# Values, indexer keys and head weights in one step of 336 columns, and wider indexer visits, in a two-layer streaming encoder

## Chip, cores and metric

The kernel runs on one core of one Trainium2 chip. The metric is the device time of one execution in microseconds (us), of which three runs were taken. The engines are named as in the profile: PE is TensorE, PEld its weight loads, DVE is VectorE, ACT is ScalarE, SP issues the loads and stores.

## What is computed

The program is one inference step of an encoder with two layers, for 256 tokens of a prompt and 8 x 16 sample tokens that share the weights (384 tokens). Cut to what matters here:

```python
for i in range(2):                                  # layers
    z  = rmsnorm(x, norm_mix) @ w_in                # one input projection, 2048 -> all groups
    q, k, v, qi, ki, wi, gates, glu, pool = split(z)
    ki = rope(ki)                                   # indexer key: 64 columns, one per token
    qi = rope(qi)                                   # indexer queries: 16 heads of 64
    logits = einsum('qhd,sd->qhs', qi, ki) / 8
    score  = einsum('qhs,qh->qs', relu(logits), wi) / 4     # wi: 16 head weights per token
    idx = top_k(where(visible, score, -inf), topk)  # chunks of 64 tokens are causal
    o_att = attention(q, k[idx], v[idx]) * silu(g_att)
    x += concat(o_att, conv(glu), pool(pool)) @ w_out
    x += sigmoid(rmsnorm(x, norm_ple) @ w_ple_gate) * (p[i] @ w_ple_proj)
y = rmsnorm(x)                                      # k, v, ki of each layer are outputs too
```

## The kernel before, in words

**Weights in pieces.** All weights pass once through the chip, in a list of pieces of 128 partitions x 1024 columns that the loop `w_dma` sends over SP's queue. `w_split` turns each piece into two: ScalarE copies it into `whi` (line 114, fp32r, the rounded part) and VectorE subtracts that from it into `wlo` (line 115). Activations are held in the same two parts, so every product takes three matmuls, lines 238, 239 and 240 in `mm3`. `w_ahead` keeps some pieces split and loaded ahead of the one in use.

**Main steps.** `ORDER` lists the steps of a layer. Each entry is an `mstep`: 48 matmuls into one bank with the tag "mm", weights stationary, the 384 tokens (320 for the indexer queries "qi") as the moving columns, over 2 pieces. The result is read by the evacuation in `pending` after the first half of the following step. The first entry, `t0`, holds the 64 columns of ki and the 16 of wi, padded to 128; `ev_t0` (line 384) scales, rotates and stores them with the columns on the partitions. The values are another kind of step, `v_step` (line 840): here the activations are stationary and 256 columns of `w_in` move, so the result has tokens on the partitions; it takes 144 matmuls over 4 pieces and three "mm" banks (lines 851 to 853).

**What runs between.** After every half step, `pump` lets each track go on to its next `yield`. `att_gen` (line 621) is the attention: it turns wi to tokens on the partitions (two transposes and two matmuls with a constant `em` that is loaded in each layer), then takes the indexer scores in visits. In the first prompt tile (64 queries whose scores count, 128 keys) a visit is one pair of heads, in the second tile (128 queries, 256 keys) too, both on line 651; for the sample it is one of the eight requests (line 691). Each matmul has 64 rows of the array, the two heads of a pair in its two row halves, and each writes a bank of its own with the tag "sd". ScalarE takes the relu, VectorE multiplies by the head weight and adds (line 660). `conv_gen` (its taps on VectorE, line 483) is another track. Of the eight accumulation banks four carry "mm" and four "sd".

**The start.** Ahead of layer 0, `ple_proj` projects the embeddings: 4 pieces, 96 matmuls of 384 columns into "sd" banks (their inputs are `phi` and `plo`), copied out by VectorE and ScalarE in turn (line 303 is ScalarE's). The squares for the norm (`square_gen`, line 199) write buffers that held `phi` and `plo`. `stats` (line 152) adds up the squares with three small matmuls (line 156) and spreads the result with transposes (line 170); it is called on after the first two steps of `ORDER`.

**Who sets the order.** The program's order is not the order on the engines: the framework schedules each engine's list ahead of time, with a simulated timeline and the banks and buffers as limits. TensorE's list then runs strictly in that order.

## Time and profile before

| | |
|---|---|
| median of three runs (lowest to highest) | 1517.2 us (1515.77 to 1517.27) |
| the profiled execution | 1517.27 us, its span 1515.4 us |
| TensorE matmuls | busy 1493.7 us, 99% of the span, 8839 instructions |
| VectorE | busy 1000.8 us, 66% |
| ScalarE | busy 667.1 us, 44% |
| loads and stores | 216.10 MB, mean 143 GB/s |

The busy time of an engine is the time in which at least one of its instructions ran. In the rows of the timeline a matmul's duration is longer than the distance to the next one, since two overlap; the distance between starts is what a matmul costs. The chain is followed back from the last instruction to what released it, or to the instruction before it on its engine. The share of a line in the chain tells where the time lies, and the list of waits tells for what an engine stood still.

### The profile page before, as it was taken

How to read it: one execution, taken by the hardware profiler on the slowest of the kernel's cores; microseconds unless marked ns; L12 is line 12 of the kernel's file. 1: busy time of each engine (PE TensorE's matmuls, PEld its weight loads, DVE VectorE, ACT ScalarE, POOL GpSimd, SP SyncE). 2: the span in 40 equal slices, each digit the busy share in tenths (PEclk: the TensorE clock that was granted, in tenths of full speed). 3: DMA queues.
4: the chain of work that ended last, by engine and by line, in shares of the span. 5: the costliest groups of instructions: out<-in, count | busy, mean ns of one | idle time of the engine just before them, and what ended most of it. 6: DMA issues, size and time to landing. Idle time of an engine off the chain costs nothing.

```text
span 1515.4 us, 22769 instructions
## 1 busy us (share of the span) xinstructions
PE 1493.7 (99%) x8839; PEld 1449.6 (96%) x8839; DVE 1000.8 (66%) x1775; ACT 667.1 (44%) x1163; POOL 3.6 (0%) x36
## 2 busy tenths in 40 slices
PE   8999999999999999999999999999999999999995
PEld 8999999999999999999999999999999999999995
DVE  7887979767466444466678797978655654445554
ACT  7653333347543333444445334344554343345441
POOL 0000000000000000000000000000000000000000
PEclk9999999999999999999999999999999999999997
DMA  9654443433446444455454444443344644444432
GB/s 339 207 154 132 149 130 113 137 110 98 135 150 205 126 126 128 132 181 175 152 172 153 134 144 129 127 138 112 98 119 131 201 137 131 128 125 125 126 111 84
DMA packets 84684, 216.10 MB, mean 143 GB/s; under 512 B 11232, under 2 KB 40800, under 8 KB 84576
## 3 DMA queue, kind: packets, MB, share of 16 engines
q1 hardware_dynamic: 84576, 214.65, 45.8%
q8 instruction: 69, 1.13, 0.3%
q14 instruction: 39, 0.32, 0.1%
HBM read 200.70 MB, written 13.91 MB: 142 GB/s over the span
## 4 chain that ended last, share of the span: by engine, by line
PE 98%; DVE 1%; ACT 1%; DMA 0%; SPq 0%; issue 0%; DVEq 0%
PE mm L238 29%; PE mm L240 29%; PE mm L239 29%; PE sd L651 1%; PE sd L238 1%; PE sd L240 1%; PE sd L239 1%; PE mm L851 1%; PE mm L852 1%; PE mm L853 1%; PE sd L715 1%; PE sd L742 1%; PE sd L691 1%; DVE xr L998 0%; DMA wraw<-in_wpp_dram 0%; PE sd L779 0%
## 5 line engine op out<-in xcount | busy, mean ns | idle before, releaser
L114 ACT ACTIVATE whi<-wraw 128x1024 fp32r<-128x1024 f32 (+1 forms) x341 | 357.7, 1050 | 631.6 <-PE mm L239 469.7
L115 DVE TENSOR_TENSOR wlo<-wraw,whi 128x1024 fp32r<-128x1024 f32 (+1 forms) x341 | 412.9, 1211 | 229.6 <-ACT whi L114 227.6
L238 PE MATMUL mm<-xh,whi 128*128 128x384 f32 (+1 forms) x752 | 252.5, 336 | 0.5 <-ACT whi L114 0.5
L238 PE MATMUL mm<-nh,whi 128*128 128x384 f32 (+1 forms) x752 | 252.4, 336 | 0.0
L240 PE MATMUL mm<-nh,wlo 128*128 128x384 f32 (+1 forms) x752 | 250.5, 333 | 0.0
L240 PE MATMUL mm<-xh,wlo 128*128 128x384 f32 (+1 forms) x752 | 250.5, 333 | 0.0
L239 PE MATMUL mm<-nl,whi 128*128 128x384 f32 (+1 forms) x752 | 249.2, 331 | 0.0
L239 PE MATMUL mm<-xl,whi 128*128 128x384 f32 (+1 forms) x752 | 248.9, 331 | 0.0
L238 PE MATMUL mm<-ph,whi 128*128 128x384 f32 x512 | 171.4, 335 | 0.0
L240 PE MATMUL mm<-ph,wlo 128*128 128x384 f32 x512 | 171.0, 334 | 0.0
L239 PE MATMUL mm<-pl,whi 128*128 128x384 f32 x512 | 171.0, 334 | 0.0
L239 PE MATMUL mm<-cl,whi 128*128 128x384 f32 x512 | 171.0, 334 | 0.0
L240 PE MATMUL mm<-ch,wlo 128*128 128x384 f32 x512 | 171.0, 334 | 0.0
L238 PE MATMUL mm<-ch,whi 128*128 128x384 f32 x512 | 170.7, 334 | 0.0
L483 DVE SCALAR_TENSOR_TENSOR ca<-u,cst,ca 128x384 f32<-128x384 f32 x240 | 147.3, 614 | 3.1
L238 PEld LDWEIGHTS mm<-xh,whi 128*128 128x128 f32 x752 | 141.2, 188 | 6.4 <-issue 4.1
L238 PEld LDWEIGHTS mm<-nh,whi 128*128 128x128 f32 x752 | 141.2, 188 | 5.5 <-issue 4.1
L240 PEld LDWEIGHTS mm<-nh,wlo 128*128 128x128 f32 x752 | 141.2, 188 | 1.2 <-issue 0.6
L239 PEld LDWEIGHTS mm<-nl,whi 128*128 128x128 f32 x752 | 141.2, 188 | 1.1 <-issue 0.8
L240 PEld LDWEIGHTS mm<-xh,wlo 128*128 128x128 f32 x752 | 141.2, 188 | 1.2 <-issue 0.6
L239 PEld LDWEIGHTS mm<-xl,whi 128*128 128x128 f32 x752 | 141.2, 188 | 1.0 <-issue 0.8
L239 PEld LDWEIGHTS mm<-pl,whi 128*128 128x128 f32 x512 | 96.1, 188 | 0.0
(221 smaller groups left out, 1850.1 us busy)
## 6 DMA issues: line engine op xcount, KB each, us to landing
wraw<-in_win_dram SPq DMA_DIRECT2D x196, 512.0 KB, 3.7
wraw<-in_wout_dram SPq DMA_DIRECT2D x64, 512.0 KB, 3.6
wraw<-in_wple_dram SPq DMA_DIRECT2D x64, 512.0 KB, 3.6
wraw<-in_wpp_dram SPq DMA_DIRECT2D x7, 512.0 KB, 4.2
x<-in_xT_dram SPq DMA_DIRECT2D x16, 192.0 KB, 5.6
pp_dram<-t SPq DMA_DIRECT2D x16, 192.0 KB, 4.9
xr<-in_xT_dram SPq DMA_DIRECT2D x16, 192.0 KB, 5.8
ppt<-pp_dram SPq DMA_DIRECT2D x16, 192.0 KB, 4.0
```

The source lines that it names most:

```text
L114: A.activation(hi[:, c], r[:, c], AF.Copy)
L115: V.tensor_tensor(lo[:, c], r[:, c], hi[:, c].bitcast(F32), OP.subtract)
L238: T.matmul(ps, hi_w, hx, start=first, stop=False)
L239: T.matmul(ps, hi_w, lx, start=False, stop=False)
L240: T.matmul(ps, lo_w, hx, start=False, stop=last)
L483: V.scalar_tensor_tensor(av, u[:, :, j:j + 16], w, av, OP.mult, OP.add)
L651: T.matmul(pss[j][r, :nk], qi[t][h, c], kiT[h, :nk], start=True, stop=True)
L691: T.matmul(pss[j][:, :KS], qis[h, b].rearrange("p t j -> p (t j)"), kb[h], start=True, stop=True)
L715: T.matmul(o, q[2 * hp + i][:, 128 * qt:128 * qt + 128], kT[g][:, :nk], start=True, stop=False)
L742: T.matmul(ps.rearrange("p (i c) -> p i c", i=4), Vt[:, kt, 128 * g:128 * g + 128], pt[:, kt], start=(kt == 0), stop=(kt == qt))
L851: T.matmul(outs[i], xh[:, c], wh, start=(k == 0), stop=False, skip_group_check=True)
L852: T.matmul(outs[i], xh[:, c], wl, start=False, stop=False, skip_group_check=True)
```

## The change

- `t0` and `v` leave `ORDER`. At the head of each layer `first_step` computes ki, wi and v together: 336 columns of `w_in` move past stationary activations, 144 matmuls, in six pieces of 3, 3, 3, 3, 2 and 2 blocks of 128 rows, into three "sd" banks. `stats` is called on after its third and fourth piece.
- The result has tokens on the partitions. Its evacuation scales by token, rotates ki with a table of its own (`tabt`, a new load), and takes wi as it stands. `ev_t0` is gone; `att_gen` now brings ki back with three transposes, and gets the sample's weights by two matmuls with a constant `batch` (8 columns more in `cst`) in place of `em` and a reduction.
- First prompt tile: two visits of four head pairs. Two heads of queries fill the two column halves of the array, so eight matmuls of 64 x 64 go into four banks a visit; the two column halves' sums are added at the end.
- Second tile and sample: visits of two pairs, four banks each.
- "mm" banks 4 to 3, "sd" banks 4 to 5.

The diff, cut to its core; of the preparation and the visits only the new text stands here, as the old one is shown above:

```diff
-ORDER = ([("t0", 0), ("gb", 0), ("ga", 0)] + [("qi", t) for t in range(8)] + [("gb", 1), ("ga", 1), ("v", 0)]
+ORDER = ([("gb", 0), ("ga", 0)] + [("qi", t) for t in range(8)] + [("gb", 1), ("ga", 1)]
          + [("pi", g) for g in (3, 2, 1, 0)] + [("k", 0), ("k", 1), ("gb", 2), ("ga", 2)] + [("q", h) for h in range(4)]
          + [("gb", 3), ("ga", 3)] + [("q", h) for h in range(4, 8)]
          + [("gp", g) for g in range(4)] + [("gc", g) for g in range(4)] + [("gt", h) for h in range(8)])
+
+
+FIRST = 336
+FIRST_K = (3, 3, 3, 3, 2, 2)
...
     def bank(tag):
-        return psum.tile([128, 512], F32, name=tag, tag=tag, bufs=4)
+        return psum.tile([128, 512], F32, name=tag, tag=tag, bufs=3 if tag == "mm" else 5)
...
+            tabt = tmp().rearrange("p (s i c) -> p s i c", s=2, i=3)
+            S.dma_start(out=tabt, in_=I["tabt"])
...
+                kr, kw = R["kr"], R["kw"]
 
                 ps = bank("sd")
+                for i in range(3):
+                    T.transpose(ps[:, 128 * i:128 * i + 128], kr[:, i].rearrange("p d c -> p (d c)"), ident)
+                A.activation(kiT, ps[:, :N], AF.Copy)
+                ps = bank("sd")
+                w2s = mt([128, 2, 8, TS], "rp", bufs=2, name="w2")
                 for j in range(2):
+                    w2 = w2s[:, j]
+                    V.scalar_tensor_tensor(w2, kw[:, 2, 64 + j:80:2, None].to_broadcast([128, 8, TS]), 1.0 / 32,
+                                           place[:, None, :].to_broadcast([128, 8, TS]), OP.mult, OP.mult)
+                    T.matmul(ps[:, NB * j:NB * j + NB], w2.rearrange("p t j -> p (t j)"), batch, start=True, stop=True)
+                V.tensor_copy(wi_s.rearrange("p a b -> p (a b)"), ps[:, 0:2 * NB])
...
+                def relu(ps, nk):
+                    rl = mt([128, 512], "rp", bufs=2, name="rl")
+                    for j in range(2):
+                        A.activation(rl[:, j * nk:j * nk + nk], ps[j][:, :nk], AF.Relu)
+                    return rl
+                def weigh(acc, rl, nk, w, first):
+                    for j in range(2):
+                        if first and j == 0:
+                            V.tensor_scalar(acc, rl[:, :nk], w(j), None, OP.mult)
+                        else:
+                            V.scalar_tensor_tensor(acc, rl[:, j * nk:j * nk + nk], w(j), acc, OP.mult, OP.add)
+                nk = 128
+                acc = mt([128, TP], "sc", bufs=2)[:, :nk]
+                for u in (0, 2):
+                    pss = []
+                    for v in (u, u + 1):
+                        ps = [bank("sd") for _ in range(2)]
+                        for a in range(2):
+                            for j in range(2):
+                                h = slice(64 * j, 64 * j + 64)
+                                T.matmul(ps[j][64 * a:64 * a + 64, :nk], qi[2 * v + a][h, 0:64], kiT[h, :nk],
+                                         start=True, stop=True)
+                        pss.append(ps)
+                    for v in (u, u + 1):
+                        weigh(acc, relu(pss[v - u], nk), nk, lambda j: wi_2[:, v, j:j + 1], v == 0)
+                    yield
+                half = mt([128, TP], "sc", bufs=2, name="half")
+                A.activation(half[64:128, :nk], acc[0:64], AF.Copy)
+                acc = acc[64:128]
+                V.tensor_tensor(acc, acc, half[64:128, :nk], OP.add)
+                G.memset(maskp[0][0:64, 0:64], 0.0)
+                G.memset(maskp[0][0:64, 64:128], OFF)
...
+                for t in range(0, 8, 2):
+                    pss = []
+                    for i in range(2):
+                        ps = [bank("sd") for _ in range(2)]
                         for j in range(2):
                             h = slice(64 * j, 64 * j + 64)
+                            T.matmul(ps[j][:, :nk], qi[t + i][h, 64:192], kiT[h, :nk], start=True, stop=True)
+                        pss.append(ps)
+                    for i in range(2):
+                        weigh(acc, relu(pss[i], nk), nk,
+                              lambda j: wi_tok[:, 2 * (t + i) + j:2 * (t + i) + j + 1], t + i == 0)
                     yield
+                V.memset(acc[0:64, nk - 64:nk], NEG)
+                yield from topk(acc, 64)
+                V.tensor_scalar(maskp[1], acc, TAKEN, OFF, OP.not_equal, OP.mult)
...
+                for b in range(0, NB, 2):
+                    nxt = [load_ki(b + 2 + i) for i in range(2)] if b + 2 < NB else None
+                    pss = []
+                    for i in range(2):
+                        ps = [bank("sd") for _ in range(2)]
+                        for j in range(2):
+                            h = slice(64 * j, 64 * j + 64)
+                            T.matmul(ps[j][:, :KS], qis[h, b + i].rearrange("p t j -> p (t j)"), kbs[i][h], start=True,
+                                     stop=True)
+                        pss.append(ps)
+                    for i, rl in enumerate(before):
+                        add_s(b - 2 + i, rl)
...
-            def v_step(gate):
-                outs = [bank("mm")[:, 0:256] for _ in range(3)]
-                for pc in range(4):
+            def first_step():
+                outs = [bank("sd")[:, :FIRST] for _ in range(3)]
+                k0 = 0
+                for pc, kn in enumerate(FIRST_K):
                     w_ahead()
                     hi, lo = w_next()
                     for i in range(3):
                         c = slice(128 * i, 128 * i + 128)
-                        for j in range(4):
-                            k = 4 * pc + j
-                            wh, wl = hi[:, 256 * j:256 * j + 256], lo[:, 256 * j:256 * j + 256]
+                        for j in range(kn):
+                            k = k0 + j
+                            wh, wl = hi[:, FIRST * j:FIRST * j + FIRST], lo[:, FIRST * j:FIRST * j + FIRST]
                             xh, xl = xs[k]
-                            T.matmul(outs[i], xh[:, c], wh, start=(k == 0), stop=False, skip_group_check=True)
-                            T.matmul(outs[i], xh[:, c], wl, start=False, stop=False, skip_group_check=True)
-                            T.matmul(outs[i], xl[:, c], wh, start=False, stop=(k == KD - 1), skip_group_check=True)
-                    if pc == 0:
-                        run_pending(gate)
-                    if pc % 2 == 1:
-                        pump()
+                            T.matmul(outs[i], xh[:, c], wh, start=(k == 0), stop=False)
+                            T.matmul(outs[i], xh[:, c], wl, start=False, stop=False)
+                            T.matmul(outs[i], xl[:, c], wh, start=False, stop=(k == KD - 1))
+                    k0 += kn
+                    pump()
+                    if pc in (2, 3):
+                        next(stat_track, None)
 
                 def ev():
+                    kw = R["kw"] = tmp()[:, :240].rearrange("p (i c) -> p i c", i=3)
+                    kr = R["kr"] = tmp().rearrange("p (i d c) -> p i d c", i=3, d=2)
                     for i in range(3):
-                        A.activation(Vt[:, i, :], outs[i], AF.Copy, scale=R["col"][:, i:i + 1])
+                        A.activation(kw[:, i], outs[i][:, 0:80], AF.Copy, scale=R["col"][:, i:i + 1])
+                    for i in range(3):
+                        A.activation(Vt[:, i], outs[i][:, 80:], AF.Copy, scale=R["col"][:, i:i + 1])
+                    scale_tab(0)
+                    for i in range(3):
                         S.dma_start(out=O["v"][l, i], in_=Vt[:, i, :])
-                    flags.add("v")
+                    ki = kw[:, :, 0:64]
+                    t = mt([128, 2, 3, 64], "gth", name="krt")
+                    a, b = t[:, 0], t[:, 1]
+                    V.tensor_tensor(a, ki, tabt[:, 0], OP.mult)
+                    V.tensor_tensor(b[:, :, 0:32], ki[:, :, 32:64], tabt[:, 1, :, 0:32], OP.mult)
+                    V.tensor_tensor(b[:, :, 32:64], ki[:, :, 0:32], tabt[:, 1, :, 32:64], OP.mult)
+                    V.tensor_tensor(kr[:, :, 0], a, b, OP.add)
+                    A.activation(kr[:, :, 1], kr[:, :, 0], AF.Copy)
+                    S.dma_start(out=O["kidx"][l], in_=kr[:, :, 0])
+                    V.tensor_scalar(wi_tok, kw[:, 1, 64:80], 1.0 / 32, None, OP.mult)
+                    for a in range(2):
+                        V.tensor_scalar(wi_2[64 * a:64 * a + 64],
+                                        kw[64:128, 0, 64:80].rearrange("p (u a j) -> p u a j", u=4, a=2)[:, :, a],
+                                        1.0 / 32, None, OP.mult)
+                    flags.add("first")
...
             stat_track = stats(ss, D, R)
+            first_step()
             for n, (kind, i) in enumerate(ORDER):
                 if n == POOL_AT:
                     pool_mm()
                 if n == CONV_AT:
                     conv_mm()
-                if kind == "v":
-                    v_step(gate)
-                    continue
                 if kind == "ga":
                     pre_ga(i)
                 mstep(xs, evs[kind](i), gate, CHUNK if kind == "qi" else 0)
-                if n < 2:
-                    next(stat_track, None)
```

The scheduler's lists show what the engines get. First the list of TensorE in the first prompt tile of the first layer; lines 238 to 240 (after the change 244 to 246) are the main stream, line 651 (658) the indexer's scores, and xh, xl the activations. Before:

```order
L239 MATMUL mm<-xl_7_253,whi 128x384
L240 MATMUL mm<-xh_7_252,wlo 128x384
L651 MATMUL sd<-kiT,qi_2_412 64x128 x2
L238 MATMUL mm<-xh_8_310,whi 128x384
L239 MATMUL mm<-xl_8_311,whi 128x384
```

And with the change:

```order
L245 MATMUL mm<-xl_7_253,whi 128x384
L246 MATMUL mm<-xh_7_252,wlo 128x384
L658 MATMUL sd<-kiT,qi_0_413 64x128 x2
L658 MATMUL sd<-kiT,qi_1_414 64x128 x2
L658 MATMUL sd<-kiT,qi_2_415 64x128 x2
L658 MATMUL sd<-kiT,qi_3_416 64x128 x2
L244 MATMUL mm<-xh_8_310,whi 128x384
```

One visit of two matmuls has become one of eight, and there are two such visits instead of eight.

In the second tile and the sample part the same list, with the change, has these two places (line 681 the second tile, 718 the sample):

```order
L246 MATMUL mm<-xh_7_252,wlo 128x384
L681 MATMUL sd<-kiT,qi_6_419 128x256 x2
L681 MATMUL sd<-kiT,qi_7_420 128x256
L244 MATMUL mm<-xh_8_310,whi 128x384
...
L245 MATMUL mm<-xl_11_323,whi 128x384
L681 MATMUL sd<-kiT,qi_7_420 128x256
L246 MATMUL mm<-xh_11_322,wlo 128x384
...
L718 MATMUL sd<-kib,qis 128x144 x2
L244 MATMUL mm<-xh_0_170,whi 128x384
L245 MATMUL mm<-xl_0_171,whi 128x384
L718 MATMUL sd<-kib,qis 128x144 x2
```

The second half of the last pair of the second tile stands 11 main matmuls behind the first, and in the sample part the two pairs of a visit are parted by two main matmuls; before, each pair of the second tile stood in one place.

Last the list of ScalarE at the start of layer 0, where t (line 303, then 309) is the copy that frees a bank of the embeddings' projection, whi the split of a piece and sq the squares. Before:

```order
L178 ACTIVATE xh_8_310<-x_302,cst 128x384
L178 ACTIVATE xh_9_314<-x_304,cst 128x384
L114 ACTIVATE whi<-wraw 128x1024
L303 ACTIVATE t<-sd 128x384
L178 ACTIVATE xh_10_318<-x_306,cst 128x384
```

And with the change:

```order
L184 ACTIVATE xh_8_310<-x_302,cst 128x384
L184 ACTIVATE xh_9_314<-x_304,cst 128x384
L205 ACTIVATE sq_476<-x_164 128x384
L205 ACTIVATE sq_485<-x_232 128x384
L205 ACTIVATE sq_482<-x_168 128x384
L118 ACTIVATE whi<-wraw 128x1008
L205 ACTIVATE sq_479<-x_166 128x384
L309 ACTIVATE t<-sd 128x384
L205 ACTIVATE sq_488<-x_234 128x384
L184 ACTIVATE xh_10_318<-x_306,cst 128x384
```

Four squares now stand ahead of that copy.

## Rows read from the trace of the kernel before

**Rows 1.** The page's busy times, its TensorE clock in 40 slices, and its chain's engines

```profile
PE 1493.7 (99%) x8839; PEld 1449.6 (96%) x8839; DVE 1000.8 (66%) x1775; ACT 667.1 (44%) x1163; POOL 3.6 (0%) x36
...
PEclk9999999999999999999999999999999999999997
...
PE 98%; DVE 1%; ACT 1%; DMA 0%; SPq 0%; issue 0%; DVEq 0%
```

**Rows 2.** TensorE's waits, longest entry: us in total, times, longest

```profile
PE sd L238 <- ACT whi L114: 4.5, 2, 4.1
```

**Rows 3.** TensorE's timeline: start us, duration us, engine, line, operation

```profile
38.20 0.33 PE L238 MATMUL mm<-xh,whi 128*128 128x384 f32 x1
...
46.52 0.33 PE L238 MATMUL mm<-xh,whi 128*128 128x384 f32 x1
...
128.30 0.28 PE L851 MATMUL mm<-whi,xh 128*128 128x256 f32 x1
...
135.84 0.28 PE L851 MATMUL mm<-whi,xh 128*128 128x256 f32 x1
```

**Rows 4.** TensorE's timeline in narrow windows, first prompt tile

```profile
150.58 0.33 PE L651 MATMUL sd<-kiT,qi 64*64 64x128 f32 x2
...
150.74 0.28 PE L651 MATMUL sd<-kiT,qi 64*64 64x128 f32 x2
...
155.33 0.33 PE L651 MATMUL sd<-kiT,qi 64*64 64x128 f32 x2
```

**Rows 5.** TensorE's timeline in narrow windows, second prompt tile

```profile
176.72 0.49 PE L651 MATMUL sd<-kiT,qi 64*128 64x256 f32 x2
...
177.04 0.38 PE L651 MATMUL sd<-kiT,qi 64*128 64x256 f32 x2
...
181.75 0.49 PE L651 MATMUL sd<-kiT,qi 64*128 64x256 f32 x2
```

**Rows 6.** TensorE's timeline in narrow windows, sample part

```profile
237.42 0.34 PE L240 MATMUL mm<-xh,wlo 128*128 128x384 f32 x1
237.69 0.39 PE L691 MATMUL sd<-kib,qis 64*128 64x144 f32 x2
...
237.91 0.29 PE L691 MATMUL sd<-kib,qis 64*128 64x144 f32 x2
...
238.41 0.34 PE L239 MATMUL mm<-xl,whi 128*128 128x384 f32 x1
```

**Rows 7.** TensorE's timeline, a sample attention's matmuls in 128 x 64 tiles

```profile
386.03 0.34 PE L779 MATMUL sd<-kkb,qas 128*64 128x144 f32 x2
```

**Rows 8.** TensorE's timeline around the preparation, and a piece of the chain (transposes)

```profile
58.57 0.31 PE L240 MATMUL mm<-xh,wlo 128*128 128x320 f32 x1
...
60.12 0.31 PE L238 MATMUL mm<-xh,whi 128*128 128x320 f32 x1
...
327.63 0.44 PE sd L736 x4
```

**Rows 9.** The start: timelines of TensorE and ScalarE; table of stretches (PE first)

```profile
18.37 0.34 PE L240 MATMUL sd<-phi,wlo 128*128 128x384 f32 x1
...
20.00 0.34 PE L239 MATMUL sd<-plo,whi 128*128 128x384 f32 x1
...
0.00:18.50 18.50, 13.90 (x60) 13.06 (x60) 10.77 (x19) 12.26 (x22) 0.68 (x11) 1.00 0.89 302
...
23.72 1.07 ACT L114 ACTIVATE whi<-wraw 128x1024 fp32r<-128x1024 f32 x1 [0.73 <-DMA wraw<-in_win_dram]
...
30.77 1.77 ACT L199 ACTIVATE sq<-x 128x384 f32<-128x384 f32 x4 [0.75 <-PE sd L239]
```

**Rows 10.** VectorE's groups, and stretch 148 to 182 (third busy time is VectorE's)

```profile
L660 DVE SCALAR_TENSOR_TENSOR sc<-rl,wi_tok,sc 128x256 f32<-128x256 f32 x30 | 14.4, 480 | 0.8
L483 DVE SCALAR_TENSOR_TENSOR ca<-u,cst,ca 128x384 f32<-128x384 f32 x240 | 147.3, 614 | 3.1
...
148.00:182.00 34.00, 34.00 (x198) 32.33 (x198) 32.41 (x68) 10.18 (x16) 0.50 (x5) 1.00 0.46 135
```

More of the change, by code (lines that the diff above doesn't have):

```diff
@@ L108, in w_split @@
             w_dma(i + 1)
-            n = pieces[i][1] * 128
+            n = pieces[i][1]
             r = raw.pop(i)
@@ L128, in w_ahead @@
         w_dma(i + PARTS - 1 + RAWS)
-    cst = const.tile([128, 752], F32, name="cst")
+    cst = const.tile([128, 760], F32, name="cst")
     ident = cst[:, 0:128]
@@ L135, in hybrid_kernel @@
     vecs = cst[:, 384:384 + 2 * 184]
+    place = selw[:, 112:128]
+    batch = cst[:, 752:760]
     ones = const.tile([128, 128], F32, name="ones")
@@ L277, in hybrid_kernel @@
     w_dma(2)
-    S.dma_start(out=cst[:, 384:], in_=I["cst"][:, 384:])
+    S.dma_start(out=cst[:, 384:752], in_=I["cst"][:, 384:752])
     for k in range(2):
@@ L314, in hybrid_kernel @@
     S.dma_start(out=cst[:, :384], in_=I["cst"][:, :384])
+    S.dma_start(out=cst[:, 752:], in_=I["cst"][:, 752:])
     V.tensor_copy(identb, ident)
@@ L616, in topk @@
                             yield
-            em = mt([128, 384], "rp", bufs=2, name="em")
-            S.dma_start(out=em, in_=I["em"])
             def att_gen():
-                while "t0" not in flags:
+                while "first" not in flags:
                     yield
+                yield
+                kr, kw = R["kr"], R["kw"]
                 ps = bank("sd")
-                for i in range(2):
-                    T.transpose(ps[:, 16 * i:16 * i + 16], wiT[:, 128 * i:128 * i + 128], ident[0:16, 0:16])
-                for j in range(2):
-                    T.matmul(ps[:, 128 + 128 * j:256 + 128 * j], em[0:16, 128 * j:128 * j + 128], wiT[:, TP:],
-                             start=True, stop=True)
-                V.tensor_copy(wi_tok.rearrange("p a b -> p (a b)"), ps[:, 0:32])
-                w2 = mt([128, 2, 128], "rp", bufs=2, name="w2")
-                V.tensor_tensor(w2, ps[:, 128:384].rearrange("p (j c) -> p j c", j=2),
-                                em[:, None, 256:384].to_broadcast([128, 2, 128]), OP.mult)
-                V.tensor_reduce(wi_s.rearrange("p a b -> p (a b)"),
-                                w2.rearrange("p j (b c) -> p (j b) c", b=NB), axis=AX, op=OP.add)
@@ L681, in add_s @@
                              stop=(b == NB - 1))
-                kb = load_ki(0)
+                kbs = [load_ki(b) for b in range(2)]
                 yield
-                before = None
-                for b in range(NB):
-                    nxt = load_ki(b + 1) if b + 1 < NB else None
-                    pss = [bank("sd") for _ in range(2)]
-                    for j in range(2):
-                        h = slice(64 * j, 64 * j + 64)
-                        T.matmul(pss[j][:, :KS], qis[h, b].rearrange("p t j -> p (t j)"), kb[h], start=True, stop=True)
-                    if before is not None:
-                        add_s(b - 1, before)
-                    rl = mt([128, 512], "rp", bufs=2, name="rls")
-                    for j in range(2):
-                        V.tensor_scalar(rl[:, j * KS:j * KS + KS], pss[j][:, :KS], 0.0,
-                                        wi_s[:, j, b:b + 1], OP.max, OP.mult)
-                    V.tensor_tensor(rl[:, :KS], rl[:, :KS], rl[:, KS:2 * KS], OP.add)
-                    before, kb = rl, nxt
+                before = []
@@ new lines, in att_gen @@
+                for b in range(0, NB, 2):
[10 more added lines that the diff above has]
+                        add_s(b - 2 + i, rl)
+                    before = []
+                    for i in range(2):
+                        rl = mt([128, 512], "rp", bufs=2, name="rls")
+                        for j in range(2):
+                            V.tensor_scalar(rl[:, j * KS:j * KS + KS], pss[i][j][:, :KS], 0.0,
+                                            wi_s[:, j, b + i:b + i + 1], OP.max, OP.mult)
+                        V.tensor_tensor(rl[:, :KS], rl[:, :KS], rl[:, KS:2 * KS], OP.add)
+                        before.append(rl)
+                    kbs = nxt
@@ L700, in att_gen @@
                     yield
-                add_s(NB - 1, before)
+                for i, rl in enumerate(before):
+                    add_s(NB - 2 + i, rl)
                 flags.add("idx")
@@ L1011, in _constants @@
         c[p, 128 + 112 + p % 16] = 1
-    for h in range(16):
-        t, j = divmod(h, 2)
-        em[h, 128 * j + 16 * t:128 * j + 16 * t + 16] = 1
-    em[:, 256:384] = (r[:, None] % 16 == r[None, :] % 16)
     c[:, 368:384] = f(1) / (np.arange(16) + 1).astype(f)
```

124 lines of the change are left out of this document (44 added, 80 removed).

## The prediction

> **What bounds the kernel.** First the page's busy times and its chain: TensorE is busy 99% of the span, and 98% of the chain that ended last is TensorE [rows 1]. Then the list of what TensorE waited for: its longest entry, 4.5 us, lies in the first microseconds, before the first weights are split [rows 2]. So from 20 us to the last layer's end TensorE's own queue is the time, and every change is priced by what it takes out of that queue or puts into it. VectorE (66%) and ScalarE (44%) count only where TensorE would have to wait for them. Last, the timeline of TensorE around each place that the change touches gives the prices. The sum is made against the profiled execution, 1517.27 us (1515.4 us of span and 1.9 us around it); the median of the runs, 1517.2 us, is the same within 0.1 us.
>
> **The first step (both layers).** A matmul of 384 columns starts every 0.1733 us (48 between the two rows, 8.32 us), one of 256 columns every 0.1197 us (63, 7.54 us) [rows 3]. Removed per layer: t0, 48 x 0.1733 = 8.32 us, and v, 144 x 0.1197 = 17.24 us. Added: 144 of 336 columns. No row has 336; on the straight line between the two rows (0.0536 us for 128 columns) one costs 0.1733 - 48 x 0.00042 = 0.1532 us. The rows bound it by 0.1197 and 0.1733, that is 17.2 and 25.0 us a step; I take the line, since both ends are the same fp32r stream with a fresh weight load each time. 144 x 0.1532 = 22.06 us. Saved: **3.50 us a layer**.
>
> **Indexer visits.** A visit interrupts the main stream with small fp32 matmuls. Three places give its price. In the first prompt tile (64 queries, 128 keys) two visits with 24 mains between them stand 4.75 us apart, so a visit costs 4.75 - 24 x 0.1733 = 0.59 us; its two passes start 0.16 us apart, and each pass is two records that run side by side (two in 0.33 us) [rows 4]. So 2 x 0.16 is work and 0.27 us is entry and exit. Second tile (256 keys): 5.03 - 4.16 = 0.87 us, a pass 0.32, entry 0.23 [rows 5]. Sample: from the main at 237.42 to the one at 238.41 there are 0.99 us with two mains in it, so the visit costs 0.65 us with 0.22 a pass and 0.21 entry [rows 6].
>
> The order on TensorE tells how often each is paid, alike in both layers. First tile: 8 visits of one head pair become 2 of four pairs. The four matmuls of a step use four quarters of the array (two row halves by two column halves). Row halves run side by side [rows 4], and so do column halves: two in 0.34 us, the length of one [rows 7]. Taken as four at once, a visit has four passes: 0.27 + 4 x 0.16 = 0.91, twice 1.82 against 8 x 0.59 = 4.72, saved 2.90 us. With the column halves one after the other it has eight passes, 3.10 in all, saved 1.62. Had each matmul to wait for the one before it in the program, its second pass included, the 8 matmuls would be 16 passes: 2 x 0.27 + 32 x 0.16 = 5.66, a loss of 0.94. I take four at once, as each pair of halves has a row of its own, and keep the other two for the range.
>
> The Trainium skill, "TensorE: Matmul & The Clock Gate", Part 3 (What overlaps and what doesn't), says that matmuls start and end strictly in program order; read literally, that is the last of these three. The trace does not agree for two halves, since both first passes run before either second one; no run here shows four.
>
> Second tile: 8 entries with 16 passes become 5 entries with 18, since the order tears one pair in two halves 11 mains apart, which no longer run side by side: 8 x 0.87 = 6.96 against 5 x 0.23 + 18 x 0.32 = 6.91. Saved 0.05: what a merged entry saves the half pair pays back. Sample: 10 entries with 20 passes, since two pairs were split, become 8 with 18, since only the first of the four visits kept its two pairs together: 6.50 against 8 x 0.21 + 18 x 0.22 = 5.64, saved 0.86. Preparation: from 58.57 to 60.12 there are 1.55 us with four mains (0.147 each at 320 columns, by the same line), so it costs 0.96 us; now three transposes and two matmuls of two passes are seven full-width records at 0.11 (four in 0.44), 0.77, saved 0.19 [rows 8]. Together **4.0 us a layer**, and 7.5 with the first step: 15.0 us for both.
>
> **The start (once).** Before, TensorE alternated the projection of the embeddings with the first steps, and lost 0.94 us at 18.37 (1.63 us to 20.00 for four matmuls worth 0.69) [rows 9]. Now all 96 projection matmuls come first. 60 had started by 18.5 us [rows 9], so the last would start at 18.37 + 36 x 0.1733 = 24.6. The first step's first bank is freed by a copy on ScalarE that the new order puts behind three squares, a split and a fourth square. The squares write where the projection's inputs lie, so they wait for TensorE's last matmuls, as the row of squares shows (its releaser is TensorE) [rows 9]. The first can start when the 92nd matmul, begun at 23.9, is through its 0.33: 24.25. A square takes 0.44 of the four's 1.77, and they start about 0.42 apart; the split takes 1.07 less 0.1 of overlap; the copy is taken like a square: 24.25 + 3 x 0.42 + 0.97 + 0.42 + 0.44 = 27.4. TensorE is ready at 24.8: a wait of about 2.7 us takes the place of 0.94. Net **loss 1.8 us**. Ends: nothing lost and 0.9 gained if the copy is not in fact late; at worst the wait lets the clock fall, as the page's clock row does only at the end of the run, where TensorE stands still before the last sums [rows 1]. Each us at 1.2 GHz costs half a us; I allow 2 us for it.
>
> **What costs nothing.** Six pieces of weights a layer as before, two of them shorter, so splits and loads fall slightly. The small table and the 8 extra constant columns are two short DMAs on SP's queue, behind x and the first pieces, needed 20 us later; a piece that lands that much later would still be ahead of its split. Three "mm" banks instead of four: a step's bank is read half a step later, so two are in use; the cover is gone if an evacuation is over 8 us late. ScalarE and VectorE do fewer, wider relus and multiplies. The values are ready earlier, and nothing waits for them.
>
> **Sum.** 1517.27 - 15.0 + 1.8 = 1504.1, rounded to **1504 us**.
>
> **Rivals.**
> A. No wait at the start, because ScalarE reaches the copy in time: 15.0 + 0.9 saved, 1501.4. For it: only 0.94 us were lost there before; against it: the squares' wait for TensorE is in the rows [rows 9].
> B. Banks. Each visit now takes four of five "sd" banks, and they come back through two relus that need the multiplies of the visit before (two output tiles). In the second tile the new order has 15 VectorE instructions between two visits: four multiplies at 0.48, four conv taps at 0.614, a split taken as ScalarE's 1.07, six others at the stretch's mean, 32.41 / 68 = 0.477: 8.3 us [rows 9, 10]. TensorE brings a visit every 24 x 0.1733 + 0.23 + 4 x 0.32 = 5.7 us. Over three gaps VectorE falls 7.9 us behind; the buffered visit covers 5.7, so 2.2 us a layer leak out: 1508.5. Against it: the half pair that the order has put 11 mains later meets just this.
> B2. The slower case: VectorE comes into that stretch already late by more than one visit; it was busy 32.41 of 34 us there before [rows 10], and 17 us of TensorE work (v) no longer lie between. Then the cover is gone and all 7.9 us a layer appear: 1504.1 + 15.8 = 1520. It decides when VectorE's lag passes 5.7 us.
> C. Column halves in turn: 2 x 1.28 more, 1506.7; every pass in program order: 2 x 3.84 more, 1511.8.
> D. The change does not merge what it says: in the sample part that is already so in the order, and is in the sum.
>
> The Trainium skill, "TensorEngine Tiling", PSUM Bottleneck, warns that packing speeds TensorE up but not the evacuation; by that rule B or B2 holds. The trace of before, with two of four banks a visit, shows no such wait [rows 2].
>
> **Numbers.** Forecast 0.64, A 0.10, B 0.10, B2 0.05, C 0.11 (0.08 and 0.03). The range 1501 to 1511 leaves out B2, the last of C and a little on the low side. A difference under 0.2% (3 us) can't be told from none. Faster by more: everything but B2 and some of B's worse part, 0.92; within 0.2%: 0.03; slower: 0.05.
>
> **What would show it.** First-step matmuls 0.153 us apart; visits of the first tile near 0.9 us with passes 0.16 to 0.17 apart; five entries in the second tile; one wait of TensorE for ScalarE near 25 us, of 2 to 3 us. Wrong if TensorE waits for banks between 150 and 260 us (B), if a first-tile visit takes over 1.4 us (C), or if the start shows no wait (A).

## The result, and the profile after

| | before | changed |
|---|---|---|
| median (lowest to highest) | 1516.75 us (1515.77 to 1517.27) | 1503.68 us (1502.22 to 1503.99) |
| profiled execution, span | 1517.27, 1515.4 us | 1503.99, 1501.5 us |
| ratio of the times | | 0.9913, 95% interval 0.9896 to 0.993 |

Each has four runs; the medians lie 13.1 us apart. The page of the changed kernel still shows one engine, TensorE, as the time (compare [rows 1]):

```profile
PE 1477.6 (98%) x8745; PEld 1443.1 (96%) x8745; DVE 987.5 (66%) x1767; ACT 660.0 (44%) x1153; POOL 3.6 (0%) x36
...
PE 97%; DVE 1%; DMA 0%; ACT 0%; issue 0%; SPq 0%; DVEq 0%; ACTq 0%
```

TensorE's list of waits (us in total, times, longest) has two new entries, both at the start: L883 is the first step's first matmul, waiting for a copy on ScalarE, and L244 with L311 an embedding projection that waits for a copy on VectorE. There is none in the visits.

```profile
PE sd L244 <- ACT whi L118: 4.4, 2, 4.1
PE sd L162 <- DVE ss L206: 3.5, 1, 3.5
PE sd L883 <- ACT t L309: 2.5, 1, 2.5
PE sd L176 <- DVE st_y L172: 1.3, 1, 1.3
PE sd L244 <- DVE t L311: 0.8, 1, 0.8
```

**Layer 1** tells what the change is worth without the start. From its first matmul to the first of the output projection (ch), in the timeline of TensorE, the kernel before:

```profile
752.61 0.33 PE L238 MATMUL mm<-nh,whi 128*128 128x384 f32 x1
...
1212.32 0.33 PE L238 MATMUL mm<-ch,whi 128*128 128x384 f32 x1
```

and the changed one:

```profile
747.83 0.31 PE L883 MATMUL sd<-whi,nh 128*128 128x336 f32 x1
...
1198.83 0.33 PE L244 MATMUL mm<-ch,whi 128*128 128x384 f32 x1
```

That is 459.71 us against 451.00, 8.71 less. This stretch is called the body of layer 1 below. The same stretch of layer 0, from TensorE's first matmul on, went from 481.24 to 476.48, only 4.76 less; so the start lost 3.95 us. What TensorE does behind the bodies takes the same time in both (267.3 us for the output projection and gate of layer 0).

**The visits**, in the timeline of TensorE, with the main matmul ahead of and behind the first one. The first visit has 16 records, in four passes of four; a narrower window shows the first four:

```profile
130.51 0.34 PE L246 MATMUL mm<-xh,wlo 128*128 128x384 f32 x1
130.78 0.67 PE L658 MATMUL sd<-kiT,qi 64*64 64x128 f32 x16
131.38 0.44 PE L244 MATMUL mm<-xh,whi 128*128 128x384 f32 x1
...
130.78 0.34 PE L658 MATMUL sd<-kiT,qi 64*64 64x128 f32 x4
...
153.22 1.14 PE L681 MATMUL sd<-kiT,qi 64*128 64x256 f32 x8
...
169.54 1.13 PE L681 MATMUL sd<-kiT,qi 64*128 64x256 f32 x6
...
172.72 0.70 PE L681 MATMUL sd<-kiT,qi 64*128 64x256 f32 x2
...
196.63 0.76 PE L718 MATMUL sd<-kib,qis 64*128 64x144 f32 x8
...
201.69 0.52 PE L718 MATMUL sd<-kib,qis 64*128 64x144 f32 x4
```

The price of a visit is what lies between the two mains beyond one main's pace, and the 0.1 us by which the first main behind it is slow: 131.38 - 130.51 - 0.17 + 0.10 = 0.80 us for the first one (0.57 for the single pair of [rows 4] by the same count). The second tile's whole visit costs 1.27, the one of three matmuls 1.26, the half pair 0.83, as much as a pair did [rows 5]. A half pair saves nothing. In the sample part a whole visit costs 0.90 and each parted pair 0.64.

**The start.** TensorE's timeline: two gaps, and then matmuls of 336 columns 0.28 us apart (28.53 to 28.81) until 31.03; later they are 0.1545 apart (101 steps from 31.18 to 46.78).

```profile
18.93 0.34 PE L246 MATMUL sd<-phi,wlo 128*128 128x384 f32 x1
20.09 0.44 PE L244 MATMUL sd<-phi,whi 128*128 128x384 f32 x1 [0.82 <-DVE t L311]
...
25.29 0.34 PE L246 MATMUL sd<-phi,wlo 128*128 128x384 f32 x1
28.08 0.65 PE L883 MATMUL sd<-whi,xh 128*128 128x336 f32 x1 [2.46 <-ACT t L309]
28.53 0.48 PE L884 MATMUL sd<-wlo,xh 128*128 128x336 f32 x1
28.81 0.48 PE L885 MATMUL sd<-whi,xl 128*128 128x336 f32 x1
...
31.18 0.32 PE L885 MATMUL sd<-whi,xl 128*128 128x336 f32 x1
...
46.78 0.32 PE L884 MATMUL sd<-wlo,xh 128*128 128x336 f32 x1
```

ScalarE at the same time: the squares start when TensorE's last projections are through, and the copy that frees the bank ends just ahead of 28.08.

```profile
24.96 1.35 ACT L205 ACTIVATE sq<-x 128x384 f32<-128x384 f32 x3 [1.57 <-PE sd L245]
26.22 1.02 ACT L118 ACTIVATE whi<-wraw 128x1008 fp32r<-128x1008 f32 x1
27.15 0.51 ACT L205 ACTIVATE sq<-x 128x384 f32<-128x384 f32 x1
27.56 0.47 ACT L309 ACTIVATE t<-sd 128x384 f32<-128x384 f32 x1
```

The table of stretches gives the granted clock behind that wait (the number ahead of the last two): 0.50 of full speed, 1.2 GHz.

```profile
28.20:30.80 2.60, 2.60 (x10) 2.60 (x11) 2.57 (x6) 2.60 (x6) 0.00 (x0) 0.50 1.05 378
```

The total, against the terms of the prediction (layer 1; the start from the two layers' difference):

| term, us | predicted | measured |
|---|---|---|
| first step, a layer | 3.50 | 3.28 (25.56 - 144 x 0.1547) |
| first tile | 2.90 | 2.93 (8 visits 4.52, now 2 x 0.80) |
| second tile | 0.05 | 0.74 (8 x 0.83, now 5.91) |
| sample | 0.86 | 1.03 (scores 6.44 to 5.20, their sums 1.98 to 2.19) |
| preparation | 0.19 | 0.18 |
| not assigned (slow first mains behind visits, of which there are fewer) | 0 | 0.55 |
| a layer | 7.5 | 8.71 |
| start, once | -1.8 | -3.95 |

Two layers less the start make 13.5 us. What follows the body of layer 1 took 0.4 us less too, and what lies outside the span 0.6 us more (2.5 against 1.9), which leaves the 13.3 us between the two profiled executions.

### The profile page after: what moved, and what is told of

Its sections match the earlier page's. It is cut to its first block, busy times and chain, and to the rows that moved or that the text cites. A ratio compares the mean times of both kernels' runs of the same rounds, so it can differ in the third digit from the quotient of the medians.

```text
span 1501.5 us, 22560 instructions
## 1 busy us (share of the span) xinstructions
PE 1477.6 (98%) x8745; PEld 1443.1 (96%) x8745; DVE 987.5 (66%) x1767; ACT 660.0 (44%) x1153; POOL 3.6 (0%) x36
## 4 chain that ended last, share of the span: by engine, by line
PE 97%; DVE 1%; DMA 0%; ACT 0%; issue 0%; SPq 0%; DVEq 0%; ACTq 0%
PE mm L244 29%; PE mm L246 29%; PE mm L245 29%; PE sd L883 1%; PE sd L885 1%; PE sd L884 1%; PE sd L244 1%; PE sd L245 1%; PE sd L246 1%; PE sd L748 1%; PE sd L775 1%; PE sd L681 1%; PE sd L718 1%; DVE xr L1046 0%; DMA wraw<-in_wpp_dram 0%; PE sd L810 0%
## 5 line engine op out<-in xcount | busy, mean ns | idle before, releaser
L118 ACT ACTIVATE whi<-wraw 128x1024 fp32r<-128x1024 f32 (+3 forms) x341 | 356.4, 1046 | 585.9 <-PE mm L245 426.6
L119 DVE TENSOR_TENSOR wlo<-wraw,whi 128x1024 fp32r<-128x1024 f32 (+3 forms) x341 | 411.4, 1207 | 223.5 <-ACT whi L118 221.1
L244 PE MATMUL mm<-xh,whi 128*128 128x384 f32 (+1 forms) x736 | 245.9, 334 | 0.0
L244 PE MATMUL mm<-nh,whi 128*128 128x384 f32 (+1 forms) x736 | 245.8, 334 | 0.0
L246 PE MATMUL mm<-xh,wlo 128*128 128x384 f32 (+1 forms) x736 | 244.9, 333 | 0.0
L246 PE MATMUL mm<-nh,wlo 128*128 128x384 f32 (+1 forms) x736 | 244.8, 333 | 0.0
L245 PE MATMUL mm<-xl,whi 128*128 128x384 f32 (+1 forms) x736 | 243.9, 331 | 0.0
L245 PE MATMUL mm<-nl,whi 128*128 128x384 f32 (+1 forms) x736 | 243.9, 331 | 0.0
L244 PE MATMUL mm<-ph,whi 128*128 128x384 f32 x512 | 171.4, 335 | 0.0
L244 PE MATMUL mm<-ch,whi 128*128 128x384 f32 x512 | 170.7, 334 | 0.0
L244 PEld LDWEIGHTS mm<-nh,whi 128*128 128x128 f32 x736 | 138.2, 188 | 3.1 <-issue 1.8
L244 PEld LDWEIGHTS mm<-xh,whi 128*128 128x128 f32 x736 | 138.2, 188 | 3.1 <-issue 1.8
```

The lines of the kernel that those rows point to most:

```text
L118: A.activation(hi[:, c], r[:, c], AF.Copy)
L119: V.tensor_tensor(lo[:, c], r[:, c], hi[:, c].bitcast(F32), OP.subtract)
L244: T.matmul(ps, hi_w, hx, start=first, stop=False)
L245: T.matmul(ps, hi_w, lx, start=False, stop=False)
L246: T.matmul(ps, lo_w, hx, start=False, stop=last)
```

## The experiments

Two questions stood behind the hit: do the terms stand for themselves, as the sum took them, and what makes the start's loss? "Theory" is in each case the table's reading. The diffs are cut to the lines that matter, and the remarks behind # are added. In all runs below but the seventh (one round) the times come from five rounds beside the kernel before, whose median was 1517.0 to 1517.1 us.

### 1. The first step alone

```diff
-                for u in (0, 2):                     # and the other merged visits
+                for qt in range(2):                  # the visits of before
```

> The first step of 336 columns stays, the visits are the old ones (one pair, one request a time). Theory (the gain is 3.3 us a layer from the step, 4.7 us a layer from the visits, and the start loses 3.95 us): two steps 6.6, preparation 0.4, the start loses 3.95, so about 3 us faster than before, 1513.5 us, 10 us slower than the change. Rival (the step with the earlier values and five banks is what brings the time, the visits are hidden): about 1504 us. In the trace: 144 matmuls 0.155 us apart, and visits at the old prices of 0.57 and 0.83 us.

Measured: 1532.99 us, ratio 1.0108 (1.0092 to 1.0123): **slower than before by 16 us**, where either theory had it faster. The body of layer 1 took 466.2 us, though the step's matmuls ran at 0.1547 us and the visits cost 11.2 and 5.07 us, as priced. The list of waits names the place:

```profile
PE sd L784 <- DVE vbn L779: 4.5, 2, 2.2
...
PE mm L244 <- DVE mxs L773: 3.9, 6, 0.7
...
PE sd L727 <- ACT lnt L505: 2.5, 2, 1.2
...
PE sd L794 <- ACT t L787: 2.4, 6, 0.4
```

All belong to the sample's attention (scores on L768, softmax, transposes on L784, values on L794) and the work beside it. Its timeline on TensorE, and the granted clock of the stretch behind:

```profile
398.21 0.34 PE L246 MATMUL sd<-yh,wlo 128*128 128x384 f32 x1
398.38 0.24 PE L766 MATMUL sd<-masks,selh 128*128 128x144 bf16 x1
398.55 0.47 PE L768 MATMUL sd<-kkb,qas 128*64 128x144 f32 x4
401.26 0.30 PE L784 MATMUL sd<-cst,pps 128*128 128x128 f32 x1 [2.24 <-DVE vbn L779]
...
403.00:406.50 3.50, 3.50 (x14) 3.50 (x14) 2.05 (x6) 1.44 (x5) 0.00 (x0) 0.52 0.42 143
```

The first request's scores come behind the 48 matmuls of the convolution's pointwise step (yh), and nothing stands between them and the transposes that need their softmax. In the kernel before the same scores, at 386.03 [rows 7], came ahead of that step:

```profile
386.43 0.45 PE L238 MATMUL sd<-yh,whi 128*128 128x384 f32 x1
```

So the attention is one turn late (a turn is one `pump`, every half step). `v_step` was not only 17 us of matmuls. It also gave the attention two turns behind the queries. The six turns that the new step gives at the head of the layer come before the attention can use them. Counted in the kernels' own loops, the first request falls one turn behind the convolution's step in this experiment alone; in all the other kernels here it falls in the same turn, ahead of it.

### 2. The prompt visits alone

```diff
-                    for t in range(8):               # in the kernel before, with t0 and v
+                    for u in (0, 2):                 # first tile: four pairs a visit
+                for t in range(0, 8, 2):             # second tile: two pairs a visit
```

> The kernel before with only the two prompt tiles' visits merged, four mm and four sd banks, t0, v and the sample part as before. Theory (a visit is paid by entries and passes as the changed trace shows: 0.80 us for eight matmuls of 64 x 64, 1.27 us for two pairs at 256 keys): a layer 2 x 0.80 + 4 x 1.27 = 6.7 instead of 11.2, so 9.0 us in all, 1507.7 us. Rival (four banks a visit leave none over, so TensorE waits for the relus): 1512 to 1518 us, with waits of TensorE at the visits of the second tile.

Measured: 1505.26 us, ratio 0.9923 (0.991 to 0.9935). No wait at a visit, with four "sd" banks of which each visit takes all. Body of layer 1: 453.5, 6.2 less. The prompt visits account for 4.52 of it, as priced (2 x 0.80 and 4 x 1.27). Another 1.28 came where nothing was edited: the sample's visits, torn into ten entries before (6.44 us), now had eight (5.16). Nearly the whole gain of the change is here already, without the first step.

### 3. The squares into other buffers

```diff
-            q = buf("B", "hl"[k % 2], 8 + k // 2 % 2, f"sq{k}", F32)
+            q = buf("B", "hl"[k % 2], 12 + k // 2 % 2, f"sq{k}", F32)
```

> The change with the squares written to two other pairs of buffers, which are free from the start, so they wait for no matmul. Theory of the prediction (the copy that frees the first step's bank is late because squares that wait for TensorE stand ahead of it): the wait near 25 us and the ten matmuls at half rate behind it go, 2.6 + 1.3 us, so 1499.8 us. Rival (ScalarE has too much to do ahead of that copy, whatever the squares wait for; its list now has ten squares ahead of it instead of four): the wait stays at 2 to 4 us, 1503 to 1505 us.

Measured: 1502.64 us, ratio 0.9906 (0.9892 to 0.9919), 1 us less than the change. The waits moved. TensorE's timeline:

```profile
19.68 0.44 PE L244 MATMUL sd<-phi,whi 128*128 128x384 f32 x1 [0.70 <-DVE t L311]
...
22.19 0.44 PE L244 MATMUL sd<-phi,whi 128*128 128x384 f32 x1 [1.21 <-DVE t L311]
...
28.45 0.42 PE L883 MATMUL sd<-whi,xh 128*128 128x336 f32 x1 [1.71 <-ACT t L309]
```

The squares no longer wait, but ten of them stand ahead of that copy instead of four, and it started at 27.91 us, later than in the change (27.56). The rival's time came: in this list ScalarE has no idle time between 15 and 32 us, and its work alone makes the copy late. It does not follow that the squares' wait did nothing in the change, since the list is another one. The half rate is gone, with three shorter waits in the place of a short and a long one; number 7 shows that it can be gone without that.

### 4. The step in "mm" banks in layer 0

```diff
-                outs = [bank("sd")[:, :FIRST] for _ in range(3)]
+                outs = [bank("mm" if l == 0 else "sd")[:, :FIRST] for _ in range(3)]
```

> The change with the first step of layer 0 alone in the three mm banks, which no copy has to free; TensorE's list then alternates embedding projections and the first step. Theory (the start's loss is the wait for a bank plus the half rate behind it): the one wait of 2.5 us and the matmuls at 0.28 us go, 1503.7 - 3.9 = 1499.8 us, at best 1499 if the 0.8 us wait near 20 us goes too. Rival (at the start the loads and splits of weights and x set the pace, so the idle time only moves): waits of the same sum for wraw, whi or xh, and 1503 to 1504 us.

Measured: 1505.47 us, ratio 0.9925 (0.9913 to 0.9938); against the change 1.8 us more. The wait for the copy is gone, and a new one stands in the list, for the norm's sums, of which 1.3 us at the program's end are old:

```profile
PE sd L176 <- DVE st_y L172: 4.4, 2, 3.1
```

The rival again, though the wait is for the sums and not for weights or x: the idle time moved to the next consumer. Behind it the clock was granted at 0.50 for longer, from 51.9 to 57.7 us.

### 5 and 8. Turns, or parts that add up?

The first experiment left two readings: the attention lacks turns (A), or the step brings a loss of its own (B). Number 5 keeps the step and merges the first tile alone, which frees six turns; number 8 keeps all old visits and gives four turns.

```diff
+                if kind == "pi":                     # number 8
+                    att_track.step()
```

> The first step of 336 columns and the first prompt tile's visits merged; second tile and sample visits as before. Theory A (the attention gets one turn every half step; the first step takes turns away that stood behind the queries, so with the old visits the attention ends in the open at the layer's end, and the six turns that the merged first tile gives back put it under cover again): body of layer 1 near 451.5 us, no waits of TensorE in the sample's attention, and 1505 us. Theory B (the parts simply add up, and the step alone loses what the last experiment showed): 1533.0 - 2 x 2.95 = 1527 us.

> The first step with all the old visits, as in the first experiment, and four extra turns for the attention: one more after each of the four pool input steps. Theory A (turns): the waits in the sample's attention go, body of layer 1 near 451.0 + 2.95 + 0.74 = 454.7 us less a little where two visits fall together, and 1511 us. Theory B (it is the old visits with five sd and three mm banks, or the values' early place, that slow the attention): still over 1525 us.

Measured: 1504.39 us (ratio 0.9914, 0.99 to 0.9927) and 1508.71 us (0.9943, 0.9929 to 0.9956); bodies of layer 1 451.9 and 454.05. The bodies are A's within 0.7 us, the times within 2.3, and both lie over 16 us from B. The first request stands ahead of yh again, as number 8's timeline shows:

```profile
373.07 0.47 PE L768 MATMUL sd<-kkb,qas 128*64 128x144 f32 x4
373.47 0.44 PE L244 MATMUL sd<-yh,whi 128*128 128x384 f32 x1
```

Number 5 also says what merging the second tile's and the sample's visits is worth beside the rest: 0.9 us of layer 1's body, and 0.7 us of the median, too little to be told from none.

### 7. Four visits of two banks in the first tile

```diff
-                for u in (0, 2):
+                for v in range(4):
```

> The change with the first tile in four visits of two times two heads (two banks) instead of two visits of four banks. Price list from the trace of the change: a visit of two passes, four quarters at once, 0.57 us, as much as one of two passes with two halves; so 4 x 0.57 = 2.28 us instead of 1.59 in layer 1. The order on TensorE also changes behind it: the second tile has seven entries (two whole visits, one of three matmuls, one of a pair and three halves): 2 x 1.27 + 1.26 + 4 x 0.83 = 7.1 instead of 5.91; the sample has four whole visits: 4 x 0.90 = 3.6 instead of 5.20. Body of layer 1: 451.0 + 0.7 + 1.2 - 1.6 = 451.3 us. Rival (quarters at once cost more than halves at once): over 0.66 us a visit in the first tile.

Measured: 1503.19 us (one round), body of layer 1 451.20 us. Entry by entry: first tile 2.34 us, second 7.14, sample 3.37. One visit in the timeline, eight records:

```profile
129.13 0.45 PE L656 MATMUL sd<-kiT,qi 64*64 64x128 f32 x8
```

It costs 0.58 us, a hundredth more than one of two row halves (0.57). The price list holds, and it tells that the visits can be bought where they are cheap: this kernel lost 2.0 us a layer in the prompt tiles and won 1.8 back in the sample part, only because the visits fell on other turns.

Its start shows something more. The wait for the bank is the one of the change, 2.46 us, but the matmuls behind it ran at the full clock (1.00, 2.4 GHz):

```profile
27.74 0.42 PE L879 MATMUL sd<-whi,xh 128*128 128x336 f32 x1 [2.46 <-ACT t L309]
...
27.90:30.50 2.60, 2.60 (x18) 2.60 (x19) 2.57 (x6) 2.60 (x6) 0.00 (x0) 1.00 1.03 374
```

The same wait stands in experiments 1, 5 and 8, and there the clock behind it was 0.50 as in the change. So the 1.3 us of half rate are not a fixed price of this wait. Layer 0 took 475.09 us up to its output projection here, 475.46 in number 3 and 476.48 in the change: the 1 us that number 3 gained is no more than the half rate that it did not have.

### 6, 9 and 10. The start, and a version that beats both

Number 6 puts the step behind the first two steps of `ORDER` (those that stood behind t0 before), number 9 also calls on the norm's sums inside it and lets the evacuations that need them try after every piece, number 10 adds two idle turns ahead of the second tile.

```diff
-            first_step()
             for n, (kind, i) in enumerate(ORDER):
+                if n == 2:                           # 6
+                    first_step()
...
+                    if pc in (1, 3):                 # 9, in first_step
+                        next(stat_track, None)
...
+                for _ in range(2):                   # 10, in att_gen
+                    yield
```

> The change with the step of 336 columns put behind the first two steps of ORDER in both layers, with its six pieces moved too, and the norm's sums called on after those two steps as before; visits as in the change. Theory (the start loses 3.9 us because the step at the head needs a bank that a late copy frees and has nothing of its own to do meanwhile, as before's steps in mm banks had): body of layer 1 as in the change, 451 us, the start as before, 1499.8 us. Rival (the start is set by ScalarE's and VectorE's list, and any order on TensorE waits for it, as when the step went into the mm banks): 1503 to 1505 us.

> The step of 336 columns behind the first two steps, as in the sixth experiment, and the norm's sums called on inside it, after its second and fourth piece, instead of after the first two steps. Theory (what the sixth experiment still lost at the start are the two waits for the sums, 1.2 and 1.4 us, and seven matmuls at 1.2 GHz behind them, 0.9 us): 1503.06 - 3.5 = 1499.6 us, no wait of TensorE between 5 and 1480 us. Rival (ScalarE's and VectorE's work at the start sets it, and the wait moves on to the next consumer): within 1 us of 1503.

> The ninth experiment's kernel with two turns in which the attention does nothing ahead of the second tile; in the order the sample's four visits then keep both pairs together (four entries instead of eight), the rest stays. Theory (price list: an entry is what is paid): a layer 4 x 0.84 instead of 5.20 for the sample's scores, 1.8 us, so 3.7 us less than the ninth, about 1496 us. Rival (the turns are short, as in the first experiment: two given away put the sample's attention into the open): slower than the ninth by 5 us or more.

Measured: 1503.06 us (ratio 0.9907, 0.9894 to 0.9921), 1498.32 us (0.9877, 0.9862 to 0.9891) and 1494.43 us (0.9851, 0.9835 to 0.9868). Number 6 came out at its rival's time. It moved the wait once more, to the sums, as its timeline shows:

```profile
42.41 0.83 PE L163 MATMUL sd<-ones,ss 128*128 128x1 f32 x6 [1.20 <-DVE ss L207]
...
44.64 0.90 PE L177 MATMUL sd<-cst,st_y 128*128 128x128 f32 x3 [1.40 <-DVE st_y L173]
```

With the sums called later in TensorE's list (number 9), only the waits at the two ends are left. The table of stretches from 4 to 60 us (span, then TensorE's busy time): the kernel before, the change, and number 9.

```profile
4.00:60.00 56.00, 54.93 (x306) 53.32 (x307) 43.51 (x73) 38.71 (x66) 0.00 (x0) 1.00 0.89 309
```

```profile
4.00:60.00 56.00, 52.30 (x291) 50.95 (x292) 42.37 (x77) 38.01 (x69) 0.00 (x0) 0.97 0.91 314
```

```profile
4.00:60.00 56.00, 55.79 (x317) 54.79 (x318) 45.09 (x76) 39.45 (x67) 0.00 (x0) 1.00 0.92 315
```

Busy 52.30 us with a clock of 0.97 in the change, 55.79 at 1.00 here. ScalarE and VectorE did more in number 9's stretch, not less: they had room, so "their work sets the start" is not the whole cause either. What number 9 changed is what TensorE has in its list while they work. Number 10 then has four whole visits in the sample part, such as this one:

```profile
199.63 0.76 PE L721 MATMUL sd<-kib,qis 64*128 64x144 f32 x8
```

Its sample scores cost 3.37 us a layer instead of 5.20, and the body of layer 1 fell from 451.00 to 449.03 us. Two turns given away cost nothing, where one turn too few cost 11 us a layer. By the count in the loops there was slack for them: in the change the attention has some eight turns with nothing to do before the first heads' queries are there, in experiment 1 none. Number 10 is 9.2 us below the change and 22.6 below the kernel before.

## Why the prediction was right, and where only the total was

**The time** (1504.0 against 1503.7 us) and the range held, but two errors of over 2 us stood against each other: the layers gave 17.4 us instead of 15.0, and the start cost 3.95 instead of 1.8. That they cancelled was luck. So was it that the merged visits gave back the turns that the first step takes, for the prediction counted no turns.

**First step.** The line between 256 and 384 columns said 0.1532 us; it was 0.1547, 0.2 us a step. What failed is the sentence on the values, "The values are ready earlier, and nothing waits for them": it looked for data, and v also carried turns. Alone, the step makes the kernel 16 us slower (experiment 1); the turns that the merged visits give back pay for it (5 and 8). Rival B2 had seen that v's 17 us no longer lie between, but asked it of VectorE's lag in the second tile, where nothing happened.

**Visits.** First tile right: four quarters at once, 0.80 a visit against 0.91 predicted. The prediction priced each pass at the distance between the first two, 0.32 us at 256 columns. The whole visit's four passes started at 153.22, 153.54, 153.76 and 153.97: 0.22 us for each pass behind the second. So a whole visit of the second tile costs 1.27 us, not 1.51. Over the five entries that is 1.0 us less than predicted; 0.3 of it the prediction had already given away by pricing the old pair at 0.87 instead of 0.83, and 0.7 is missing. The first passes of four matmuls run together in 0.34 us, and none waits for another one's second pass; so rival C falls. The Trainium skill, "TensorE: Matmul & The Clock Gate", Part 3 (What overlaps and what doesn't), says that matmuls start in order and end in order. It does not say that each has to end before the next starts, as the prediction's third price took it.

**Sample.** Size near (0.86 against 1.03), reason wrong: old single visits cost 5.07 to 5.17 us a layer in experiments 1, 2, 5 and 8, no more than the merged ones of the change (5.20). The 6.44 of before were two torn pairs. Merging brought nothing there until the visits fell on other turns (7 and 10).

**Start.** The mechanism was there, the wait 2.46 us against 2.7. The mis-sized steps: "takes the place of 0.94", where a gap of 0.98 us for another copy (18.93 to 20.09) stayed beside the new one; and the clock, which stood in the range alone, where ten matmuls at 0.28 us cost 1.3 us. The prediction's cause stands in the trace: ScalarE stood 1.57 us for TensorE ahead of the three squares. It is not all of it. TensorE was ready at 25.62 us and the copy ended at 28.03; by the same list without that wait it would have come some 0.8 us late all the same, an estimate from these rows. Number 3 cannot part the two, since its list is another one.

**Rivals.** A fell by the 2.46 us wait, B and B2 by the list of waits, in which nothing stands between 150 and 260 us. What experiment 1 showed, an attention that is one turn late, was on no list, and would have been the slower case of this change without the merged visits.

Left open in part: how the 11 us a layer of experiment 1 split (11.3 in layer 0 and 12.1 in layer 1 over number 8, which has the same visits). The waits named above and a fifth (0.5 us) make 6.9 us a layer. The clock was granted at 0.50 for 3.4 us behind them in layer 0 and 6.8 in layer 1, which costs at most half of that. The rest, 2 to 3 us, was not counted one by one. Open is also why the clock fell behind the wait of 2.46 us in four of these kernels and not in number 7.

## What to carry to other kernels

Where tracks get turns between the steps of a main stream, count turns as well as microseconds: a step that is moved takes its turns along, and a track that is one turn late at the end of a layer can cost more than the step saved. Price an interruption by its entry and by the pitch of its later passes, from rows of its own, and look in the order for torn ones: they cost an entry each, and moving them by a turn or two can be worth as much as merging them. A wait at the start that moves from consumer to consumer was mended here by what the bound engine has to do meanwhile (9), not by removing the wait that happened to be named (3, 4 and 6).

## What was not expected of the hardware

- Matmuls of 64 x 64 in all four quarters start together: a visit of eight records costs 0.58 us, as one of four (0.57).
- The first pass of a visit takes 0.32 us to the next at 256 columns, the later ones 0.22; at 128 columns it is 0.16 and 0.11.
- A lone half pair costs what a pair costs: 0.83 us at 256 columns, 0.64 at 144.
- The granted clock does not follow from one wait's length. Behind the wait of 2.46 us it was 0.50 for ten matmuls in the change, and 1.00 in experiment 7. It stayed at 1.00 behind waits of 0.70, 1.21 and 1.71 us in experiment 3, and fell to 0.50 behind two of 1.20 and 1.40 us close together in experiment 6.
